# The experts' result stores issued by POOL, those of the last two positions by ScalarE and SP in turn

## The chip, the cores and the metric

One core of a Trainium2 chip runs the program. The metric is the device time of one execution in microseconds, as the median of several runs. Engines are PE (TensorE), DVE (VectorE), ACT (ScalarE), POOL (GpSimd) and SP (SyncE); DMAs are issued here by SP, ACT and POOL.

## What is computed

A decoder block over 1024 tokens of width 1024 in float32: a mixer (half gMLP, half RWKV-7) between two projections, then a mixture of 32 experts in which each token takes its two best experts of its best group, then a last RMSNorm. The part that matters here:

```python
def expert_block(args):
    xbk, e = args
    return (jax.nn.silu(xbk @ w_gate[e]) * (xbk @ w_up[e])) @ w_down[e]

yb = lax.map(expert_block, (xb, block_e)).reshape(P, D)
y = jnp.zeros((N + 1, D), yb.dtype).at[tok_buf].add(yb * w_buf[:, None].astype(yb.dtype))
...
x = x + gate2[:, None, :] * y
...
return _rmsnorm(x, final_norm_g)
```

w_gate and w_up are 1024 x 512 per expert, w_down is 512 x 1024: 6.3 MB of weights for each of 32 experts.

## The kernel before

The mixer and the router take the first 785 us or so. Then comes the experts' stage, which the change touches. The experts are taken in 32 positions; position n has room for CAPS[n] groups of 32 tokens (2 to 6, 90 groups in all), and a Block is up to four groups of one position, 33 blocks in all. A loop over the positions (from L1708 on) runs for position n: weights, `gate_up` of n, `down` of n-1, `act` of n, `operand` of n+1, `gather` of n+2.

- Weights: SP loads each position's gate and up weights (L1471) and down weights (L1478), six DMAs of 1 MB, into a ring of nine tiles `wt` of 2 MB; a load waits until PE is done with the tile's old content.
- `gather` (L1548): POOL issues one indirect DMA per group, which brings token rows from `h2d` into one of three buffers `xg`.
- `operand` (L1556, L1559): DVE transposes `xg` to `xT` and applies scale and shift.
- `gate_up` (L60 by way of `mm_`, into PSUM tiles `mm`, of which there are two): PE multiplies; the groups lie side by side in the 32-column strips of the array. ACT then takes the SiLU into `sg` (L1576), and DVE multiplies it with the up part and the routing weight into `sp` (L1579).
- `act` (L1585): DVE transposes `sp` to `aT`.
- `down` (L60, into PSUM tiles `pch`, three): PE multiplies with the down weights; DVE multiplies by gate2 into one of two buffers `yo` (L1601). Then ACT issues four DMAs that store `yo` to `ysd` in DRAM (L1604), 64 to 128 KB each: 132 in all.

After the loop SP loads `x1d` into two ring tiles (L1743, eight DMAs of 512 KB). A loop for overflowing experts (L1747) follows, which has no iteration with these inputs. Then POOL gathers each token's two result rows from `ysd` with 16 indirect DMAs (L1777); DVE, ACT and POOL add, normalise and scale, and SP and ACT store the output (L1787).

The order of the instructions on each engine is set by the framework's scheduler, which runs the program through a simulated timeline (`schedule_with_timeline_sim=True`); a store may so stand elsewhere than in the code. It also chooses buffers, and gives each DMA a completion semaphore in turn out of a set of eight: DMAHW0 to 7 for the DMAs that SP and ACT issue, DMASW0 to 7 for POOL's. A DMA waits on its issuing engine until the DMA that had the same semaphore before has landed. Each engine runs its instructions in its order.

Of the kernel before, what the change touches and what calls it, by code (L numbers as in the profile page):

```python
# [28 lines left out]
NEXP = 32  # L29
# [25 lines left out]
def hybrid_block(ctx, tc, a, out):  # L55
    nc = tc.nc
    ctx.enter_context(nc.allow_non_contiguous_dma(reason="column layouts"))

    def mm_(*a_, **k_):
        nc.tensor.matmul(*a_, **k_)  # L60
# [22 lines left out]
    def c512():  # L83
        return psc.tile([P, 512], F32, name="pch")
# [164 lines left out]
    class Stream:  # L249


        def __init__(self):
            self.jobs, self.raws, self.parts = [], {}, {}
            self.nl = self.ns = 0
            self.eng = [nc.gpsimd]
            self.loads = []
# [1276 lines left out]
    class Block:  # L1533


        def __init__(self, ix, wt, ng, put):
            self.ix, self.wt, self.ng, self.put = ix, wt, ng, put

        turn = 0

# [47 lines left out]
        def down(self, w):  # L1588
            po = [c512() for _ in range(0, self.ng, 2)]
            w3 = w.rearrange("p (k f) -> p k f", k=4)  # L1590
            for k in range(4):
                for g in range(self.ng):
                    for h in range(4):
                        r = slice(32 * h, 32 * h + 32)
                        mm_(po[g // 2][r, (g % 2) * 256:(g % 2) * 256 + 256], self.aT[:, g, 32 * k:32 * k + 32],
                            w3[:, k, 256 * h:256 * h + 256], start=(k == 0 and g % 2 == 0), stop=(k == 3),
                            skip_group_check=True)
            yo = ap_.tile([P, 4, 256], F32, name="yo")
            for g0 in range(0, self.ng, 2):
                m = min(2, self.ng - g0)  # L1600
                nc.vector.tensor_tensor(yo[:, g0:g0 + m, :], po[g0 // 2][:, 0:256 * m].rearrange("p (g f) -> p g f", g=m),  # L1601
                                        gate2.unsqueeze(1).to_broadcast([P, m, 256]), op=OP.mult)
            for h in range(4):
                nc.scalar.dma_start(self.put[:, :, 256 * h:256 * h + 256], yo[32 * h:32 * h + 32, 0:self.ng, :])  # L1604

    slots = lambda r, n: ysd[r:r + 32 * n, :].rearrange("(g t) f -> t g f", t=32)

# [5 lines left out]
                self.blocks.append(Block(lambda g, g0=g0: idx[:, g0 + g, i:i + 1], lambda g, g0=g0: wrep[:, g0 + g, i:i + 1], n, slots(BASES[i] + 32 * g0, n)))  # L1613

    positions = [Position(i) for i in range(NEXP)]
    for ps_ in positions[0:2]:
        for b_ in ps_.blocks:
            b_.gather()
# [202 lines left out]
```

## Time and profile before

| | us |
|---|---|
| median of 3 runs | 1407.06 |
| lowest and highest of them | 1404.6, 1409.46 |
| the profiled execution | 1394.24 |
| its span, first to last instruction | 1392.4 |
| PE busy (matmul) | 1185.6 |
| DVE busy | 639.5 |
| POOL busy | 468.3 |
| ACT busy | 349.0 |

The profiled execution is a run of its own, 1.8 us longer than its span. Busy times are sums over the whole span, most of which the change does not touch; issuing a DMA does not count as busy time. A row with ACTq or SPq is the engine's queue at issuing DMAs: its duration covers a series of issues together with what they wait for.

### The profile page before, as it was taken

Reading aid. Unit: us, or ns where it says so; the run is one execution under the profiler, and the core shown is the slowest. Engines: PE = TensorE matmul, PEld = TensorE weight load, DVE = VectorE, ACT = ScalarE, POOL = GpSimd, SP = SyncE. Lnnn points to the kernel's source line nnn. Section 1 sums busy time; section 2 is a strip of 40 time slices with the busy share of each in tenths; the row PEclk is TensorE's granted clock in tenths of the full one; section 3 lists DMA queues with packets and bytes.
Section 4 is the critical chain, followed back from the end, with each engine's and each line's share of the span. In section 5 each row is a group of like instructions: output and inputs, shape, how many; then the busy total and the mean of one; then the engine's idle time right before and its main releaser. Section 6 shows DMA issues by size and latency. Waiting matters only on the chain. (4 is left out here: it accounts for less than half of the span.)

```text
span 1392.4 us, 35836 instructions
## 1 busy us (share of the span) xinstructions
PE 1185.6 (85%) x15245; PEld 907.4 (65%) x15245; DVE 639.5 (46%) x1569; ACT 349.0 (25%) x627; POOL 468.3 (34%) x562
## 2 busy tenths in 40 slices
PE   3888799999998899899998489998989999699730
PEld 1576687767875787789986368765657777356420
DVE  2562864793365945772247344332233322132127
ACT  2643453234353643322345200000000000000002
POOL 4464432632554424432440363221122221020025
PEclk9998869999999959899998599999999999899875
DMA  9338325353226212340059799999999999999947
GB/s 324 88 108 296 108 64 175 103 158 90 77 88 191 83 32 65 89 143 32 22 194 387 280 371 416 405 415 405 407 415 393 420 414 411 417 419 359 372 152 278
DMA packets 125139, 336.54 MB, mean 242 GB/s; under 512 B 16936, under 2 KB 77280, under 8 KB 100400
## 3 DMA queue, kind: packets, MB, share of 16 engines
q1 hardware_dynamic: 88784, 273.44, 51.8%
q0 software_dynamic: 13392, 37.63, 7.4%
q10 hardware_dynamic: 22800, 23.12, 5.0%
q8 instruction: 122, 2.00, 0.6%
q14 instruction: 41, 0.34, 0.1%
HBM read 297.98 MB, written 38.96 MB: 242 GB/s over the span
## 5 line engine op out<-in xcount | busy, mean ns | idle before, releaser
L60 PE MATMUL mm<-wt,xT 128*32 128x256 f32 x5760 | 336.0, 393 | 60.2 <-ACT sg L1576 28.1
L60 PEld LDWEIGHTS mm<-wt,xT 128*32 128x32 f32 x5760 | 227.9, 114 | 162.6 <-ACT sg L1576 51.3
L60 PE MATMUL mm<-h,w 128*128 128x512 f32 (+2 forms) x864 | 225.2, 413 | 9.7 <-ACT h L307 4.4
L1548 POOL DMA_INDIRECT xg<-h2d,idx x90 | 98.9, 1099 | 334.0 <-DVE xT L1556 309.7
L60 PEld LDWEIGHTS mm<-h,w 128*128 128x128 f32 (+2 forms) x864 | 161.5, 192 | 56.2 <-issue 6.1
L285 POOL TENSOR_TENSOR w<-wraw,w 128x512 fp32r<-128x512 f32 (+2 forms) x104 | 131.3, 1265 | 141.7 <-ACT w L283 141.2
L60 PE MATMUL pch<-wt,aT 128*32 128x256 f32 x2880 | 162.5, 379 | 2.2 <-DVE yo L1601 2.2
L1579 DVE SCALAR_TENSOR_TENSOR sp<-mm,wrep,sg 128x128 f32<-128x128 f32 x90 | 31.8, 422 | 271.5 <-ACT sg L1576 271.2
L60 PEld LDWEIGHTS pch<-wt,aT 128*32 128x32 f32 x2880 | 111.3, 110 | 46.8 <-DVE yo L1601 3.5
L1576 ACT ACTIVATE sg<-mm 128x256 f32<-128x256 f32 (+1 forms) x52 | 17.1, 354 | 489.3 <-DMA wt<-in_moe_w_up_dram 185.2
L60 PE MATMUL mm<-w,h 128*128 128x256 f32 (+1 forms) x816 | 128.0, 312 | 1.4 <-DVE aw L335 0.5
L60 PEld LDWEIGHTS mm<-w,h 128*128 128x128 f32 x816 | 113.5, 206 | 9.3 <-issue 2.9
L283 ACT ACTIVATE w<-wraw 128x512 fp32r<-128x512 f32 (+2 forms) x104 | 63.4, 615 | 107.5 <-PE mm L60 47.2
L1556 DVE STREAM_TRANSPOSE xT<-xg 128x768 f32<-128x768 f32 (+2 forms) x33 | 29.5, 894 | 89.5 <-PE mm L60 77.7
L60 PE MATMUL pch<-s,GM 16*32 16x16 f32 (+3 forms) x1280 | 53.7, 200 | 6.2 <-DVE s L672 3.4
L60 PEld LDWEIGHTS pch<-s,GM 16*32 16x32 f32 (+2 forms) x1280 | 48.6, 125 | 13.9 <-issue 6.5
L1559 DVE TENSOR_TENSOR xT<-xT,mod 128x768 f32<-128x768 f32 (+2 forms) x66 | 56.7, 859 | 0.2
L1777 POOL DMA_INDIRECT wt<-ysd,rowi x16 | 16.5, 1033 | 101.1 <-DMA ysd<-yo 96.5
L60 PE MATMUL py<-aw,ccol 128*1 128x256 f32 x320 | 28.6, 441 | 11.7 <-DMA aw<-in_ada_w_dram 11.4
L559 DVE SCALAR_TENSOR_TENSOR GM<-pch,nsq,gmask 128x128 f32<-128x128 f32 x128 | 35.2, 341 | 1.6 <-PE pch L60 1.2
L1601 DVE TENSOR_TENSOR yo<-pch,gate 128x512 f32<-128x512 f32 (+1 forms) x52 | 30.0, 608 | 11.1 <-PE pch L60 7.4
L60 PE MATMUL pch<-AR,kb 64*128 64x128 f32 x256 | 28.2, 322 | 4.5 <-DVE GM L559 3.6
(424 smaller groups left out, 1592.2 us busy)
## 6 DMA issues: line engine op xcount, KB each, us to landing
wt<-in_moe_w_gate_dram SPq DMA_DIRECT2D x64, 1024.0 KB
wt<-in_moe_w_up_dram SPq DMA_DIRECT2D x64, 1024.0 KB
wt<-in_moe_w_down_dram SPq DMA_DIRECT2D x64, 1024.0 KB
aw<-in_ada_w_dram SPq DMA_DIRECT2D x48, 512.0 KB
wraw<-in_w_in_dram SPq DMA_DIRECT2D x80, 256.0 KB
ysd<-aw POOLq DMA_DIRECT2D x1, 8192.0 KB, 28.2
ysd<-yo ACTq DMA_DIRECT2D x56, 96.0 KB
wraw<-in_w_out_dram SPq DMA_DIRECT2D x16, 256.0 KB
```

What stands on the lines that cost most here:

```text
L60: nc.tensor.matmul(*a_, **k_)
L283: nc.scalar.activation(hi, raw, AF.Copy)
L285: eng.tensor_tensor(lo, raw, hi.bitcast(F32), op=OP.subtract)
L559: nc.vector.scalar_tensor_tensor(GM[:, u, :], pgs[h][:, c * P:(c + 1) * P], nsq[:, u:u + 1], gmask, op0=OP.mult, op1=OP.mult)
L1548: tc.keep_in_program_order(nc.gpsimd.indirect_dma_start(out=self.xg[:, 256 * g:256 * g + 256], out_offset=None, in_=h2q, in_offset=bass.In ...
L1556: nc.vector.transpose(xT.rearrange("p g k t -> p (g k t)"), self.xg[:, 0:256 * self.ng])
L1559: Block.last = nc.vector.tensor_tensor(xT, xT, m_, op=op)
L1576: nc.scalar.activation(sg[:, g0:g0 + m, :], v[:, :, 0, :], AF.Silu)
L1579: nc.vector.scalar_tensor_tensor(self.sp[:, g0 + g, :].rearrange("p (b j) -> p j b", b=4), perm(v[:, g, 1, :]), self.wt(g0 + g), perm(sg[: ...
L1601: nc.vector.tensor_tensor(yo[:, g0:g0 + m, :], po[g0 // 2][:, 0:256 * m].rearrange("p (g f) -> p g f", g=m), gate2.unsqueeze(1).to_broadca ...
L1777: nc.gpsimd.indirect_dma_start(out=part(t, j), out_offset=None, in_=ysd, in_offset=bass.IndirectOffsetOnAxis(ap=rowi[:, t, j:j + 1], axis=0))
```

## The change

The stores of `yo` to `ysd` at the end of `down` (L1604 before, L1605 now) are issued by the engine that the block names in `eng`. For the blocks of positions 0 to 29 that is POOL, 124 stores. The blocks of the last two positions, 30 and 31, have none: their stores are issued by ACT and SP in turn, two each per position, and so are those of the overflow loop. Nothing else in the code changes; the scheduler makes the order anew.

```diff
@@ class Block
             self.ix, self.wt, self.ng, self.put = ix, wt, ng, put
+            self.eng = None
@@ Block.down
             for h in range(4):
-                nc.scalar.dma_start(self.put[:, :, 256 * h:256 * h + 256], yo[32 * h:32 * h + 32, 0:self.ng, :])
+                (self.eng or (nc.scalar, nc.sync)[h % 2]).dma_start(self.put[:, :, 256 * h:256 * h + 256], yo[32 * h:32 * h + 32, 0:self.ng, :])
@@ after the positions are made
     positions = [Position(i) for i in range(NEXP)]
+    for ps_ in positions[:NEXP - 2]:
+        for b_ in ps_.blocks:
+            b_.eng = nc.gpsimd
```

On ACT, the last rows ahead of the overflow loop before the change (`sg` is the SiLU, `ysd<-yo` a store; 2, 3 or 4 in the middle of its shape is the number of groups):

```order
L1604 DMA ysd<-yo 32x3x256 x4
L1576 ACTIVATE sg<-mm 128x256
L1604 DMA ysd<-yo 32x4x256 x4
L1604 DMA ysd<-yo 32x2x256 x4
L1576 ACTIVATE sg<-mm 128x256
L1576 ACTIVATE sg<-mm 128x128
L1576 ACTIVATE sg<-mm 128x256 x2
L1604 DMA ysd<-yo 32x3x256 x4
L1604 DMA ysd<-yo 32x2x256 x4
L1604 DMA ysd<-yo 32x3x256 x4
L1604 DMA ysd<-yo 32x2x256 x4
```
The same place now. The stores of positions up to 29 are gone from between the SiLUs; what is left are two of position 30:

```order
L1577 ACTIVATE sg<-mm 128x128
L1577 ACTIVATE sg<-mm 128x256 x4
L1577 ACTIVATE sg<-mm 128x128
L1577 ACTIVATE sg<-mm 128x256 x2
L1577 ACTIVATE sg<-mm 128x128
L1577 ACTIVATE sg<-mm 128x256 x2
L1605 DMA ysd<-yo 32x2x256 x2
```
What a store waits for on ACT before the change, at the eight stores in a row with a SiLU ahead and behind (the row of waits names semaphores and engines):

```order
L1576 ACTIVATE sg<-mm 128x256 [waits PE_49,Activation_49]
L1604 DMA ysd<-yo 32x4x256 [waits DMAHW4_49,DVE_49]
L1604 DMA ysd<-yo 32x4x256 [waits DMAHW5_49]
L1604 DMA ysd<-yo 32x4x256 [waits DMAHW6_49]
L1604 DMA ysd<-yo 32x4x256 [waits DMAHW7_49]
L1604 DMA ysd<-yo 32x2x256 [waits DMAHW0_49,DVE_49]
L1604 DMA ysd<-yo 32x2x256 [waits DMAHW1_49]
L1604 DMA ysd<-yo 32x2x256 [waits DMAHW2_49]
L1604 DMA ysd<-yo 32x2x256 [waits DMAHW4_49]
L1576 ACTIVATE sg<-mm 128x256 [waits PE_49,Activation_49]
```
Each has to wait for a semaphore of the set that SP's weight loads use as well. On POOL, the last rows ahead of the overflow loop were gathers alone:

```order
L1548 DMA xg_8154<-h2d,idx 128x256 x2
L1548 DMA xg_8155<-h2d,idx 128x256 x3
L1548 DMA xg_8156<-h2d,idx 128x256 x2
L1548 DMA xg_8154<-h2d,idx 128x256 x2
L1548 DMA xg_8155<-h2d,idx 128x256 x2
L1548 DMA xg_8156<-h2d,idx 128x256 x2
```
Now the stores stand between them; the stores of three more positions follow behind these rows:

```order
L1605 DMA ysd<-yo 32x3x256 x4
L1549 DMA xg_8156<-h2d,idx 128x256 x2
L1605 DMA ysd<-yo 32x4x256 x4
L1605 DMA ysd<-yo 32x2x256 x4
L1549 DMA xg_8154<-h2d,idx 128x256 x2
L1549 DMA xg_8155<-h2d,idx 128x256 x2
L1605 DMA ysd<-yo 32x3x256 x4
L1549 DMA xg_8156<-h2d,idx 128x256 x2
L1605 DMA ysd<-yo 32x2x256 x4
L1605 DMA ysd<-yo 32x3x256 x4
L1605 DMA ysd<-yo 32x4x256 x4
L1605 DMA ysd<-yo 32x2x256 x4
```
At the end of the stage DVE's last four results were these before, with their waits; the last one waits for the semaphores of the stores of position 29, whose buffer it takes:

```order
L1601 TENSOR_TENSOR yo<-pch,gate_7481 128x512 [waits DMAHW2_49,DMAHW4_49,DMAHW1_49,DMAHW0_49]
L1585 STREAM_TRANSPOSE aT<-sp 128x256 [waits DVE_49,PE_49]
L1601 TENSOR_TENSOR yo<-pch,gate_7481 128x512 [waits DMAHW6_49,DMAHW1_49,DMAHW7_49,DMAHW0_49,DVE_49]
L1601 TENSOR_TENSOR yo<-pch,gate_7481 128x256
L1601 TENSOR_TENSOR yo<-pch,gate_7481 128x512 [waits DMAHW3_49,DMAHW4_49,DMAHW2_49,DMAHW5_49,DVE_49,PE_49]
L1601 TENSOR_TENSOR yo<-pch,gate_7481 128x512 [waits DMAHW1_49,DMAHW6_49,DMAHW0_49,DMAHW7_49,DVE_49,PE_49]
```
Now those of positions 28, 29 and 30 wait for POOL's stores two positions back, and the last one waits for four semaphores of the other set, which are those of position 30's stores:

```order
L1602 TENSOR_TENSOR yo<-pch,gate_7481 128x512 [waits DMASW6_49,DMASW7_49,DMASW5_49,DMASW4_49]
L1586 STREAM_TRANSPOSE aT<-sp 128x256 [waits DVE_49,PE_49]
L1602 TENSOR_TENSOR yo<-pch,gate_7481 128x512 [waits DMASW2_49,DMASW1_49,DMASW3_49,DMASW0_49,DVE_49]
L1602 TENSOR_TENSOR yo<-pch,gate_7481 128x256
L1602 TENSOR_TENSOR yo<-pch,gate_7481 128x512 [waits DMASW5_49,DMASW6_49,DMASW4_49,DMASW7_49,DVE_49,PE_49]
L1602 TENSOR_TENSOR yo<-pch,gate_7481 128x512 [waits DMAHW1_49,DMAHW6_49,DMAHW0_49,DMAHW7_49,DVE_49,PE_49]
```
These are issued by ACT (two) and by SP, where the two stand behind the eight loads of `x1d`; each waits for the semaphore of one of those loads:

```order
L1747 DMA wt<-x1d 128x1024 [waits DMAHW6_49,PE_49]
L1747 DMA wt<-x1d 128x1024 [waits DMAHW7_49]
L1747 DMA wt<-x1d 128x1024 [waits DMAHW0_49]
L1747 DMA wt<-x1d 128x1024 [waits DMAHW1_49]
L1747 DMA wt<-x1d 128x1024 [waits DMAHW2_49,DMASW6_49,PE_49]
L1747 DMA wt<-x1d 128x1024 [waits DMAHW3_49,DMASW7_49]
L1747 DMA wt<-x1d 128x1024 [waits DMAHW4_49,DMASW0_49]
L1747 DMA wt<-x1d 128x1024 [waits DMAHW5_49,DMASW1_49]
L1605 DMA ysd<-yo 32x2x256 [waits DVE_49,DMAHW7_49,Activation_49,Pool_49]
L1605 DMA ysd<-yo 32x2x256 [waits DMAHW0_49]
```
## Rows read from the trace of the kernel before

**Rows 1.** The page, part 2: the span in 40 equal slices of 34.8 us, the DMA engines' busy tenths and the GB/s that they moved.

```profile
DMA  9338325353226212340059799999999999999947
GB/s 324 88 108 296 108 64 175 103 158 90 77 88 191 83 32 65 89 143 32 22 194 387 280 371 416 405 415 405 407 415 393 420 414 411 417 419 359 372 152 278
```

**Rows 2.** Busy time by stage, one row for a stretch (us from the span's start): its length, busy us of PE, PEld, DVE, ACT and POOL with the count of records, then granted clock, DMA share, GB/s.

```profile
810.00:1260.00 450.00, 414.51 (x7424) 294.58 (x7420) 140.95 (x274) 16.04 (x46) 102.47 (x93) 0.96 1.02 411
1060.00:1070.00 10.00, 10.00 (x192) 7.32 (x188) 4.69 (x11) 0.77 (x2) 3.13 (x4) 1.00 0.96 323
1130.00:1140.00 10.00, 10.00 (x192) 7.29 (x187) 0.00 (x0) 0.00 (x0) 0.00 (x0) 1.00 1.01 418
1260.00:1280.00 20.00, 18.49 (x334) 11.15 (x330) 7.55 (x15) 1.03 (x3) 0.00 (x0) 1.00 0.85 314
1280.00:1302.00 22.00, 17.29 (x323) 12.29 (x312) 2.04 (x4) 0.00 (x0) 0.00 (x0) 0.98 1.02 421
1302.00:1310.00 8.00, 4.69 (x45) 2.51 (x49) 3.12 (x7) 0.55 (x2) 0.00 (x0) 0.50 0.66 227
1308.00:1310.00 2.00, 2.00 (x25) 1.00 (x21) 0.00 (x0) 0.00 (x0) 0.00 (x0) 0.50 0.94 340
```

**Rows 3.** The timeline of ACT and its queue in the experts' stage: start us, duration us, engine, line, operation, out<-in, count, and in brackets the idle time before with its releaser.

```profile
1014.63 11.65 ACTq L1604 DMA_DIRECT2D ysd<-yo  x4
1026.38 0.38 ACT L1576 ACTIVATE sg<-mm 128x256 f32<-128x256 f32 x1 [16.17 <-DMA wt<-in_moe_w_up_dram]
...
1188.11 8.57 ACTq L1604 DMA_DIRECT2D ysd<-yo  x4
1196.77 0.38 ACT L1576 ACTIVATE sg<-mm 128x256 f32<-128x256 f32 x1 [21.17 <-DMA wt<-in_moe_w_up_dram]
1204.15 13.51 ACTq L1604 DMA_DIRECT2D ysd<-yo  x4
1217.76 0.55 ACT L1576 ACTIVATE sg<-mm 128x256 f32<-128x256 f32 x2 [20.60 <-DMA ysd<-yo]
...
1286.68 17.32 ACTq L1604 DMA_DIRECT2D ysd<-yo  x8
1304.10 0.55 ACT L1576 ACTIVATE sg<-mm 128x256 f32<-128x256 f32 x2 [26.14 <-DMA ysd<-yo]
...
1340.16 2.26 ACTq L1604 DMA_DIRECT2D ysd<-yo  x4
```

**Rows 4.** The timeline of PE's matmuls from 1176 us to its last one, same columns.

```profile
1176.26 7.11 PE L60 MATMUL mm<-wt,xT 128*32 128x256 f32 x128 [0.61 <-ACT sg L1576]
...
1198.03 11.65 PE L60 MATMUL mm<-wt,xT 128*32 128x256 f32 x176 [8.61 <-DVE sp L1579]
...
1218.97 15.74 PE L60 MATMUL mm<-wt,xT 128*32 128x256 f32 x256 [5.83 <-ACT sg L1576]
...
1305.31 16.94 PE L60 MATMUL mm<-wt,xT 128*32 128x256 f32 x256 [8.02 <-ACT sg L1576]
1323.99 12.29 PE L60 MATMUL pch<-wt,aT 128*32 128x256 f32 x224 [1.75 <-DVE yo L1601]
```

**Rows 5.** Who waited for whom: PE from 810 to 1345 us, then SP's queue from 1180 to 1345 us (line, who was waited for: us in total, times, longest us).

```profile
PE mm L60 <- ACT sg L1576: 28.1, 8, 8.0
PE mm L60 <- DVE sp L1579: 15.9, 5, 8.6
...
SPq L1478 <- DMA wt<-in_moe_w_down_dram: 21.5, 1, 21.5
SPq L1471 <- PE pch L60: 8.4, 1, 8.4
```

**Rows 6.** The timeline of SP's queue from 1306 us, of DVE's last result and of POOL's first gather of the last stage, same columns as in group 3.

```profile
1306.21 0.86 SPq L1478 DMA_DIRECT2D wt<-in_moe_w_down_dram  x2
1307.17 6.96 SPq L1743 DMA_DIRECT2D wt<-x1d  x8
...
1336.56 0.69 DVE L1601 TENSOR_TENSOR yo<-pch,gate 128x512 f32<-128x512 f32 x1 [2.97 <-PE pch L60]
...
1346.96 0.97 POOL L1777 DMA_INDIRECT wt<-ysd,rowi  x1 [96.49 <-DMA ysd<-yo]
```

**Rows 7.** The chain of waits that ended last, in order of time, from 1342 to 1348 us: start us, us, what.

```profile
1341.93 4.38 DMA ysd<-yo
...
1347.93 0.30 issue
```

**Rows 8.** POOL's issues by line: the gathers L1548 from 860 to 1260 us (operation, count: ns min/median/max; next row: us to landing), then the direct DMAs of 512 KB from POOL's queue at L1107 with their landings, and the stretch in which these landed, with the columns of group 2.

```profile
L1548 POOL DMA_INDIRECT xg<-h2d,idx x62: 992/1000/1742, 861.3 to 1249.1; - x62
...
DMA to landing us min/median/max: 5.7/6.8/8.2
...
L1107 POOL DMA_DIRECT2D h2d<-b x4: 531/531/576, 764.2 to 773.2; - x4
...
DMA to landing us min/median/max: 16.6/16.7/17.3
...
764.00:790.00 26.00, 16.71 (x171) 13.27 (x170) 11.98 (x72) 9.48 (x13) 3.89 (x8) 0.65 0.90 363
```

**Rows 9.** The page, part 5: PE's groups of the experts' stage (line, engine, operation, out<-in, count | busy us, mean ns of one | idle us before, releaser).

```profile
L60 PE MATMUL mm<-wt,xT 128*32 128x256 f32 x5760 | 336.0, 393 | 60.2 <-ACT sg L1576 28.1
L60 PE MATMUL pch<-wt,aT 128*32 128x256 f32 x2880 | 162.5, 379 | 2.2 <-DVE yo L1601 2.2
```

## The prediction

> **What bounds the kernel now.** The page's slices come first [rows 1]: from slice 24 (801 us) on the DMA engines are busy nine tenths or more, at 371 and then 393 to 420 GB/s; slices 37 and 38 fall to 359 and 372, the next to 152, and there the last stage begins. The busy times by stage say it closer [rows 2]: 411 GB/s from 810 to 1260 us (418 in an undisturbed stretch, some 415 between its dips), but 314 from 1260 to 1280 and 227 from 1302 to 1310. A position brings 6 weight loads of 1.049 MB, and on average 2.8 gathers of 131 KB and as many bytes of results: 7.0 MB, at 415 GB/s 16.9 us. PE has 8640 records in 32 positions [rows 9], 270 each; at 192 in 10 us [rows 2] that is 14.1 us. So the DMA stream is the limit, and PE can catch up 2.8 us per position.
>
> Then ACT and its queue [rows 3]. The four stores of a position hold ACT for 8.6 to 13.5 us, and the SiLU stands right behind them: it starts 0.1 us after the last store's issue, though its matmuls are long done. The order printed above tells why: each store waits for a semaphore DMAHW that a weight load of SP had before it. Against 0.5 us for an issue that finds its semaphore free (2.26 us for four at 1340), the rest is waiting for loads. PE pays: 28.1 us before matmuls that wait for the SiLU, 15.9 for the product behind it [rows 5]. Up to 1180 us most of this is covered by the DMA stream. From there it is not: PE stands 8.61, 5.83 and 8.02 us [rows 4], the ring of weight tiles fills, SP waits 8.4 us for PE [rows 5], and the stream has holes. At the very end eight stores in a row hold ACT 17.32 us, and SP's load of the last down weights waits 21.5 us for another load [rows 3, 5]. PE's last matmul ends at 1336.28; from the last result to the end the kernel runs a fixed chain.
>
> **The change, part by part.**
> *ACT loses 124 of 132 issues.* The SiLU then follows its matmuls. Two limits tell what this gives at the end of PE's work. PE's own: from 1176 us it loses 8.61 + 5.83 + 8.02 = 22.5 us standing, and runs slower behind each stand (the granted clock is 0.50 from 1302 to 1310 us, its level of 1.2 GHz, after the longest [rows 2]): 176 records in 11.65 us, 256 in 15.74 and 256 in 16.94 [rows 4] instead of 9.8, 14.2 and 14.2 at 55.5 ns (128 in 7.11), 6.1 us more. Together 28.6 us. The weights': the holes cost (415-323) x 10, (415-314) x 20 and (415-227) x 8, over 415: 2.2 + 4.9 + 3.6 = 10.7 us [rows 2]. The last two loads were issued from 1306.21 us on [rows 6]; 0.68 MB by 1310 at 340 GB/s and 1.42 MB at 415 make them land at about 1313.4. Without holes: 1302.7. The last gate and up weights stand 4 loads ahead, 10.1 us: 1292.6. Behind them come 64 records (3.6 us), the gap of 1.75 us for SiLU and product, and the 224 records of the last three down products (12.29 us) [rows 4]: 1310.2 instead of 1336.28, so **-26.1 us**. The smaller of the two is taken. Earlier than 1176 us nothing is counted: there the stream hides ACT.
>
> *POOL gains 124 issues.* A direct DMA takes 0.53 to 0.58 us of POOL, the gap to the next issue 0.30 us, a gather 1.00 [rows 7, 8]. Per position: 4 x 0.85, 2.8 x 1.30 and half a table scatter at a gather's price, 0.65: 7.7 us of 16.9. In the printed order stores and gathers alternate; a gather is issued some two positions ahead of its use, so a store that waits in front of it for its result holds nobody. Cost 0, hidden by POOL's idle time; if that cover goes, it is the last rival. The results are in two buffers, so DVE's result n+2 waits until store n has landed: 4 issues (up to 5.2 us, at the 1.00 us of a gather) and a landing as of a gather, 5.7 to 8.2 us [rows 8], 13 us of 34. Cost 0. The bytes stay the same, so the stream's rate does.
>
> *The last two positions.* Two issues by ACT and two by SP instead of four in a row: of 2.26 us half goes, **-1.1 us** before the gathers at 1346.96 [rows 3, 6]. Against it stands a new wait, seen in the order only: the last result now takes the buffer of the one before it, so DVE waits until the stores of position 30 have landed. SP issues its two of them behind eight loads of x1d (4.19 MB). Before, these loads were issued at 1307 to 1314 [rows 6] and long gone; now they follow the last weights directly and end at 1302.7 + 10.1 = 1312.8 us. With 2 us for the landing (between 0 and the 4.38 of the chain [rows 7]) the last result starts at 1314.8 instead of 1310.2: **+4.6 us**, bounds 0 and 8 (both issues and a full landing behind the last load). Behind that result DVE has only the last stage, which POOL starts when the stores of position 31 have landed. A faster PE so runs into transfers that it never met.
>
> Sum: -26.1 - 1.1 + 4.6 = **-22.6 us**. On the profiled execution (1394.24 us) that is 1371.6. The median of the runs is 12.8 us above it, so the difference is laid on the median: 1407.06 - 22.6 = **1384.5 us**.
>
> Here a rule speaks against it. By the rows, an issue held ACT not for the cost of issuing but for its wait. The Trainium skill, "DMA: Bandwidth & Descriptors", section "Issuing engines are not separate DMA queues", says that DMAs of all issuers share the same 16 DMA engines, and that issuing from several engines saves only the sequencer's issue time. By that rule the sum would be the -1.1 us of the last issues. The rows agree with its first half (the bytes and 415 GB/s stay); for its second half 17.32 us of ACT for eight stores is the other measure.
>
> **The rivals.**
> *Only the last stand goes.* The weights may bring PE's lateness back: SP's loads wait for semaphores in turn, and PE may stand for weights where it stood for the SiLU. Then only the 8.02 us, the 2.7 us of slow matmuls behind it and the 1.1 us go, and the last result waits for an undisturbed landing, +2.7 (a result 0.69, two issues 1.13, landing 4.38, less the 3.5 us that PE's last 64 records take anyway): -9.1 us, **1398 us**. For it: most stands before 1176 us cost nothing. Against: SP waited 8.4 us for PE, not PE for weights.
>
> *No change.* The stream ends when it ends and the last weights set the finish; the holes would be the loads' own. 1407.06 - 1.1 = **1406 us**. Against it: the holes lie where PE stood.
>
> *POOL becomes the bound, and it is slower.* POOL's DMAs take their semaphores DMASW from a set of eight, in turn; an issue waits until the DMA eight before has landed. A position has 7.2 of them (230 in 32), so POOL keeps pace while a landing takes less than 8 / 7.2 x 16.9 = 18.8 us. At 20 us a position takes 18.0, 1.1 more, in 28 positions 31 us; less the 9.1 above it is +22: **1429 us**. The place is the gather behind held stores, then DVE's transpose. For it: four direct DMAs of 512 KB landed after 16.6 to 17.3 us while loads ran beside them [rows 8]. Against: the stores have 96 KB, and gathers among saturated loads landed after 8.2 us at most. The Trainium skill, "SBUF — State Buffer", section "SBUF: two separate sides", names another way there: POOL can't write descriptors while VectorE runs a two-port operation, 620 ns becoming 3100. By that the estimate is 2.5 us more per store, 17.7 us of POOL per position, and some 1420 us; the trace's longest gather issue is 1.742 against 1.000 us [rows 8].
>
> **How the numbers follow.** The forecast has 0.68, only the last stand 0.16, no change 0.08, POOL as bound 0.08. The low end is PE's own limit without the new wait, 28.6 + 1.1: 1377.4, less 2.4 for the spread of the three runs, 1375. The high end holds the first rival with the same spread: 1400. What is left out are the last two cases. A measurement can tell 0.3% from no change, about 4 us: faster 0.84, same 0.08, slower 0.08.
>
> **What would show it.** Right: ACT's SiLUs wait for PE alone, PE's three stands after 1176 us are gone, the DMA rate stays near 415 GB/s until the last weights at about 1303 us, the last result starts near 1315 with DVE waiting for a store of position 30, and the stage of the gathers keeps its 45 us. Wrong: DVE waiting for stores in the middle of the stage, POOL's landings above 15 us, PE standing for weights after 1180 us, or a rate below 405 GB/s before it.

## The result and the profile after

The changed kernel takes **1398.33 us** (median of 8 runs, 1392.39 to 1402.11), the kernel before 1405.55 beside it (8 runs, 1400.97 to 1409.46): a ratio of **0.9937 [0.9916, 0.9958]**. It is faster, as forecast, but by 7.2 us here, and by 10.4 and 9.7 us in two later sets of runs, instead of 22.6. Four of the versions below had one execution each of 1736 to 6191 us, far above their others, which their ratios leave out.

The profiled execution of the change took 1399.25 us, 5.0 us *more* than that of before in [rows 1 to 9]. The reason is where the experts' stage starts: its first SiLU is at 816.30 us there and at 835.25 us in the change. A second profile of the kernel before starts at 832.50 us, and one of the change at 832.00, so this is a difference between executions. What sets it was not settled, but it goes with the chip: the seven profiles of groups 3 and 4 below, all from one chip, start at 813 to 820 us, the other eleven, from three chips, at 823 to 839. With the early start the kernel before also took 5 us longer from there (520.0 us from the first SiLU to PE's last matmul when it starts at 816, 515.2 us when it starts at 832). So times are counted from the first SiLU below, and the second profiles of both kernels, which start alike, are what is subtracted.

The slices of the change, as those of [rows 1]. The stage has no slice of 359 or 372 GB/s at its end any more; there is one of 380, which holds a hole that is left, then 419, in which `x1d` follows the last weights:

```profile
DMA  9338326353236202241059769999999999999965
GB/s 323 87 110 299 104 64 186 90 171 84 69 92 204 71 25 75 78 142 31 17 191 391 284 214 407 417 416 416 420 415 419 420 418 419 419 417 380 419 212 217
```

Busy time by stage in the same execution, columns as in [rows 2], then 10 us of it by themselves. POOL went from 102 us to 157 in the long stretch (on POOL, other than on SP and ACT, issuing a DMA does count as busy time). Up to 1321 us the stream moves 413 to 420 GB/s on average, with one hole in it, 288 GB/s from 1270 to 1280 us. PE's granted clock (column before the DMA share) is 1.00, 1.00, 0.92 and 1.00, and 0.83 in the hole; the 0.50 from 1302 to 1310 us, behind PE's longest stand, has no counterpart:

```profile
829.00:1279.00 450.00, 433.54 (x7680) 333.41 (x7676) 149.53 (x288) 18.23 (x49) 156.73 (x188) 1.00 1.01 414
1279.00:1299.00 20.00, 20.00 (x376) 12.03 (x372) 4.56 (x10) 0.66 (x2) 4.32 (x8) 1.00 1.01 413
1299.00:1321.00 22.00, 17.88 (x299) 11.05 (x294) 4.06 (x10) 0.77 (x2) 0.55 (x2) 0.92 1.01 420
1321.00:1329.00 8.00, 7.75 (x144) 5.17 (x136) 0.51 (x2) 0.00 (x0) 3.73 (x8) 1.00 0.96 379
```
```profile
1270.00:1280.00 10.00, 7.74 (x112) 4.37 (x116) 3.08 (x7) 0.00 (x0) 2.17 (x4) 0.83 0.76 288
```

Who waited for whom from 810 to 1345 us, ACT first, then PE, as [rows 5]. ACT's SiLU waits for PE alone. Of PE's 28.1 us for the SiLU 3.5 are left (16.9 and 4.4 in the second profiles, which start alike). Waits for `yo`, which frees a PSUM tile, grow from 2.2 us to 6.5, and waits for weights are new. "issue" is time in which PE waited for nothing that the profile shows; in the second profile of the kernel before it is 10.0 us too, so it does not come with the change:

```profile
ACT sg L1577 <- PE mm L60: 464.6, 37, 26.7
```
```profile
PE mm L60 <- issue: 10.3, 8, 2.2
PE pch L60 <- DVE yo L1602: 6.5, 3, 3.2
PE mm L60 <- DMA wt<-in_moe_w_up_dram: 4.9, 4, 2.4
PE mm L60 <- ACT sg L1577: 3.5, 3, 2.2
```

PE's last matmuls in that execution, as [rows 4]. The stands of 8.61, 5.83 and 8.02 us are gone; the longest now is 3.25:

```profile
1272.26 8.80 PE L60 MATMUL pch<-wt,aT 128*32 128x256 f32 x128 [3.25 <-DVE yo L1602]
...
1309.34 8.80 PE L60 MATMUL mm<-wt,xT 128*32 128x256 f32 x128 [2.38 <-DMA wt<-in_moe_w_up_dram]
1319.88 8.86 PE L60 MATMUL pch<-wt,aT 128*32 128x256 f32 x160 [1.74 <-DVE yo L1602]
1329.72 3.66 PE L60 MATMUL pch<-wt,aT 128*32 128x256 f32 x64 [0.98 <-PE pch L60]
```

Behind it the last results on DVE, then POOL's first gather of the last stage, as [rows 6]. The last result stands 6.45 us and starts 4.4 us behind PE's end (1333.38); before, it started 0.3 us behind it. The row books the wait to SP at the overflow loop (L1751). The semaphores that the result waits for, though, are those of position 30's four stores, and the last of these landed at 1337.65 us by its increments, just ahead of the result:

```profile
1328.93 1.02 DVE L1602 TENSOR_TENSOR yo<-pch,gate 128x512 f32<-128x512 f32 x2 [3.15 <-DMA ysd<-yo]
1330.68 0.69 DVE L1602 TENSOR_TENSOR yo<-pch,gate 128x512 f32<-128x512 f32 x1 [0.72 <-DMA ysd<-yo]
1337.82 0.69 DVE L1602 TENSOR_TENSOR yo<-pch,gate 128x512 f32<-128x512 f32 x1 [6.45 <-SPq L1751]
```
```profile
1346.22 1.04 POOL L1781 DMA_INDIRECT wt<-ysd,rowi  x1 [13.80 <-DMA ysd<-yo]
```

The pair that starts alike, kernel before and then the change: PE's last matmuls of the second profiles.

```profile
1306.29 3.66 PE L60 MATMUL pch<-wt,aT 128*32 128x256 f32 x64
1318.01 15.69 PE L60 MATMUL mm<-wt,xT 128*32 128x256 f32 x256 [8.05 <-ACT sg L1576]
1335.45 12.29 PE L60 MATMUL pch<-wt,aT 128*32 128x256 f32 x224 [1.75 <-DVE yo L1601]
```
```profile
1305.82 8.74 PE L60 MATMUL mm<-wt,xT 128*32 128x256 f32 x128 [3.27 <-DMA wt<-in_moe_w_up_dram]
1316.31 8.86 PE L60 MATMUL pch<-wt,aT 128*32 128x256 f32 x160 [1.75 <-DVE yo L1602]
1326.24 3.66 PE L60 MATMUL pch<-wt,aT 128*32 128x256 f32 x64 [1.07 <-issue]
```

PE ends at 1347.74 and 1329.90: 17.8 us earlier. The first gather comes at 1358.10 and 1342.69: 15.4 us earlier. The span ends at 1404.0 and 1394.4: only 9.6 us earlier. So 5.8 us are lost *behind* the first gather, in a stage that the change does not touch. The last waits of SP tell where (line, who was waited for: us in total, times, longest), and POOL's own row at that line what (count: ns min/median/max). Before, then the change:

```profile
SPq L1817 <- DMA out_dram<-wt: 2.2, 1, 2.2
SPq L1817 <- PEq L1817: 0.7, 2, 0.5
```
```profile
L1817 POOLq DRAIN  x3: 46/111/1817, 1398.1 to 1403.8; - x3
```
```profile
SPq L1821 <- PEq L1821: 6.6, 2, 6.0
SPq L1821 <- DMA out_dram<-wt: 2.0, 2, 1.6
```
```profile
L1821 POOLq DRAIN  x3: 46/111/10718, 1382.8 to 1394.1; - x3
```

The waits name PE's queue, which has nothing to do there. What is late is POOL: at the closing barrier its DRAIN takes 10.72 us instead of 1.82.

### The profile page after: what moved, and what is told of

Read it like the earlier page. It is cut to its first block, busy times and chain, and to the rows that moved or that the text cites. A ratio compares the mean times of both kernels' runs of the same rounds, so it can differ in the third digit from the quotient of the medians.

```text
span 1397.5 us, 35829 instructions
## 1 busy us (share of the span) xinstructions
PE 1201.7 (86%) x15245; PEld 943.3 (67%) x15245; DVE 639.1 (46%) x1569; ACT 350.4 (25%) x627; POOL 543.0 (39%) x686
## 5 line engine op out<-in xcount | busy, mean ns | idle before, releaser
L60 PE MATMUL mm<-wt,xT 128*32 128x256 f32 x5760 | 339.3, 385 | 34.7 <-DVE xT L1560 13.2
L60 PEld LDWEIGHTS mm<-wt,xT 128*32 128x32 f32 x5760 | 250.3, 111 | 112.8 <-issue 46.2
L1549 POOL DMA_INDIRECT xg<-h2d,idx x90 | 103.7, 1152 | 243.6 <-DVE xT L1557 208.4
L60 PE MATMUL pch<-wt,aT 128*32 128x256 f32 x2880 | 181.4, 382 | 9.7 <-DVE yo L1602 6.5
L60 PEld LDWEIGHTS pch<-wt,aT 128*32 128x32 f32 x2880 | 124.4, 111 | 57.8 <-issue 17.1
L60 PEld LDWEIGHTS mm<-w,h 128*128 128x128 f32 x816 | 116.3, 211 | 9.5 <-issue 3.0
L1605 POOL DMA_DIRECT2D ysd<-yo x124 | 69.2, 571 | 101.9 <-DVE yo L1602 101.8
L60 PE MATMUL py<-aw,ccol 128*1 128x256 f32 x320 | 28.1, 434 | 12.2 <-DMA aw<-in_ada_w_dram 11.9
```

Of the source, the lines that this page charges most:

```text
L1549: tc.keep_in_program_order(nc.gpsimd.indirect_dma_start(out=self.xg[:, 256 * g:256 * g + 256], out_offset=None, in_=h2q, in_offset=bass.In ...
L1605: (self.eng or (nc.scalar, nc.sync)[h % 2]).dma_start(self.put[:, :, 256 * h:256 * h + 256], yo[32 * h:32 * h + 32, 0:self.ng, :])
```

## The experiments

They ran in five groups, each beside its own runs of the kernel before (medians 1391.84 to 1406.11 us), so ratios of one group are compared. The table has, from each trace: the first SiLU of the experts, from there to the end of PE's last matmul, from that to the first gather of the last stage, from that to the end, and POOL's closing DRAIN (us). "Stores" is how many POOL issues.

| group, kernel | stores | ratio [95%] | first SiLU | to PE's end | to gather | to end | DRAIN |
|---|---|---|---|---|---|---|---|
| 1 before_again | 0 | 0.9988 [0.9964, 1.0011] | 832.50 | 515.25 | 10.36 | 45.90 | 1.82 |
| 1 after_again | 124 | 0.9904 [0.9867, 0.9940] | 832.00 | 497.90 | 12.79 | 51.71 | 10.72 |
| 1 pool_only | 124 | 0.9928 [0.9902, 0.9954] | 827.70 | 498.25 | 13.20 | 51.74 | 10.72 |
| 1 last_only | 0 | 0.9984 [0.9959, 1.0009] | 838.87 | 517.94 | 8.28 | 45.40 | 1.81 |
| 2 drain_early | 124 | 0.9926 [0.9907, 0.9945] | 831.31 | 499.49 | 16.98 | 46.12 | 1.96 |
| 2 yo31_own | 124 | 0.9921 [0.9899, 0.9943] | 836.67 | 507.36 | 4.18 | 51.59 | 10.72 |
| 2 all_pool | 132 | 0.9888 [0.9870, 0.9905] | 830.24 | 498.39 | 12.85 | 44.02 | 1.49 |
| 2 half_pool | 60 | 0.9996 [0.9981, 1.0011] | 831.32 | 516.87 | 8.58 | 46.72 | 5.90 |
| 3 late_pool | 24 | 0.9955 [0.9922, 0.9988] | 813.53 | 513.72 | 9.87 | 45.58 | 3.53 |
| 3 early_pool | 100 | 0.9993 [0.9965, 1.0022] | 817.91 | 518.83 | 8.88 | 49.68 | 8.76 |
| 3 pool31 | 128 | 0.9919 [0.9892, 0.9947] | 815.82 | 503.97 | 7.33 | 51.58 | 11.04 |
| 3 yo24_first | 124 | 0.9936 [0.9910, 0.9962] | 820.23 | 499.55 | 13.01 | 51.02 | 10.72 |
| 4 small26 | 124 | 0.9966 [0.9942, 0.9989] | 813.36 | 504.96 | 13.59 | 51.40 | 10.72 |
| 4 all_yo24 | 132 | 0.9931 [0.9903, 0.9958] | 819.81 | 501.62 | 11.67 | 45.40 | 1.49 |
| 4 pool31_yo24 | 128 | 0.9928 [0.9906, 0.9951] | 815.25 | 502.14 | 7.20 | 51.91 | 11.04 |
| 5 after_third | 124 | 0.9927 [0.9901, 0.9952] | 827.54 | 497.49 | 12.82 | 51.55 | 10.72 |
| 5 all_pool_b | 132 | 0.9899 [0.9869, 0.9929] | 823.13 | 498.32 | 12.84 | 45.92 | 1.49 |
| 5 all_yo24_b | 132 | 0.9895 [0.9866, 0.9924] | 831.70 | 500.52 | 11.86 | 45.03 | 1.49 |

### Both kernels again, and the change in halves

Two copies, and each half of the change alone:

```diff
pool_only:  (self.eng or nc.scalar).dma_start(...)   # last two positions by ACT
last_only:  b_.eng = nc.scalar                       # positions 0 to 29 by ACT
```

> The kernel before, unchanged, profiled a second time. Theory A (the profile of before that was shown began its expert stage early, and that is rare): the first SiLU of the experts now starts at 825 to 837 us instead of 816.30, the profiled time is 1401 to 1409 instead of 1394.24, and the stage from there on looks as before. Theory B (the late start of the changed kernel, first SiLU at 835.25, comes with the change): the first SiLU again at 814 to 820 us, profiled time 1392 to 1397. Timed runs: ratio 1.00 under both.

> The changed kernel, unchanged, profiled a second time. Theory A: the first SiLU lies anywhere from 816 to 837 us, and the time moves with it; PE's late arrival at the closing barrier (6.0 us in the first profile) comes and goes. Theory B: again at 833 to 837 us, with the 2 us gaps of PE between 810 and 822, and PE again 6 us late at the end. Timed runs: 1396 to 1401 us under both, 0.992 to 0.996 of before.

> POOL issues the stores of positions 0 to 29 as in the change; the stores of the last two positions are all issued by ACT, as before. If the gain comes from the 124 stores that ACT loses, nearly all of it is here: 1396 to 1402 us, between 1 us faster and 3 us slower than the change (the two issues that go back to ACT cost 1.1 us; SP's two stores behind eight x1d loads go away, up to 4.4 us back). If the gain came from the last two positions alone: 1403 to 1407 us.

> ACT and SP issue the stores of the last two positions in turn as in the change; all others stay with ACT. If the gain comes from the 124 stores: 1402 to 1409 us, the last stand halved or replaced by the wait for SP's stores. The rival, that only the last stand of PE counts: 1396 to 1400 us, as fast as the change.

The kernel before can start its stage at 832.5 us too, so the late start does not come with the change. The whole gain is POOL's half: pool_only has the change's 498 us up to PE's end, last_only before's 518. The last two positions' issues by ACT and SP are worth nothing that can be measured.

### The DRAIN and the last result

```diff
drain_early:  tc.keep_in_program_order(nc.gpsimd.drain())   # ahead of the loads of x1d
yo31_own:     yo = xgs[1]... for the last block             # a buffer of its own
all_pool:     for ps_ in positions:                         # all 132 stores by POOL
half_pool:    positions[:NEXP - 2:2] by POOL, positions[1:NEXP - 2:2] by ACT
```

> The change, with one more DRAIN of POOL right behind its last store (position 29), where POOL then waits 11 to 14 us for the gathers. In the three profiles with POOL's stores the closing DRAIN takes 10.72 us and ends 5.9 us after everything else; in the three without them 1.82 us, and it holds nobody. Theory (POOL's DRAIN has to settle the DMAs that POOL issued, once): the early one takes 8 to 11 us between 1328 and 1342, the closing one falls to about 2 us, from the first gather to the end 45.4 to 46 us instead of 51.3 to 51.7, time 1389 to 1393 us (6 us less than the change). Rival (the closing DRAIN has its length from the number of direct DMAs in the whole program, or from something else at the end): still 10.7 us, no gain, or a loss of up to 5 us if the early one delays the first gather.

> The change, with the last position's result in a tile of its own (the gather tile of position 31, which has been transposed by then) instead of the buffer of position 30's result. It tests the step of +4.6 us: the last result should then follow PE's last matmul at once instead of standing 6.4 us behind SP's branch and position 30's stores. First gather 8.0 to 9.5 us behind PE's end instead of 12.8 and 12.8: time 1391 to 1395 us. Rival (the landing of position 31's stores behind the x1d loads takes the time anyway): no change, 1396 to 1400.

> All 132 stores by POOL, the last two positions' too. Their issue stands behind no x1d load, but four issues in a row take 2.2 us on POOL against 0.9 on ACT and SP side by side. First gather 10 to 14 us behind PE's end; the closing DRAIN 11 us if its length goes with the number of direct DMAs on POOL (84 ns each), 10.7 if not. Time 1394 to 1400 us.

> POOL issues the stores of every second position of 0 to 29 (60 DMAs), ACT those of the others; the last two by ACT and SP. It asks for two doses. The closing DRAIN of POOL: about 6 us if its length goes with the number of stores on POOL, 1.8 or 10.7 if it is a matter of yes or no. PE's end behind the first SiLU (515 to 520 us with ACT, 498 with POOL): 505 to 512 if every store that ACT loses counts alike, 498 to 501 if ACT has only to be free every second position. Time 1396 to 1404 us.

drain_early: POOL's rows at its own DRAIN and at the closing one.

```profile
L1745 POOLq DRAIN  x1: 10183/10183/10183, 1329.0 to 1329.0; - x1
```
```profile
L1821 POOLq DRAIN  x3: 46/111/1962, 1388.2 to 1393.6; - x3
```

The 10 us are owed for the stores and paid once: the closing DRAIN falls to 1.96 us and the last stage to 46.12, as before. But the early one held POOL to 1339.2 us, ACT came through the overflow loop's barrier only behind POOL and issued its stores of the last position from 1342.7 us (1337.2 in the change's second profile), and the first gather came 4 us later. Net gain: none that shows, against 6 us expected.

half_pool's DRAIN (5.90 us for 60 stores) fits 72 ns per store, (10.72 - 1.82) / 124, within 0.3 us; so do late_pool, early_pool and pool31 below. Whether it goes with the stores' number or their bytes was not separated. **all_pool breaks the line**: with 132 stores it is 1.49 us. Why it falls between 128 and 132 is open. It is the one version here that keeps the change's 498 us and not its 5.8.

yo31_own took the wait for position 30's stores away, and won nothing: the scheduler then put PE's last eight records behind the empty overflow loop, whose barrier waits in its turn. SiLU to gather is 511.5 us, 511.0 in the change.

```profile
1342.95 1.08 PE L60 MATMUL pch<-wt,aT 128*32 128x256 f32 x8 [6.13 <-issue]
```

half_pool gains nothing: from the first SiLU to the first gather it takes 525.5 us, before_again 525.6. The fifteen positions whose stores stay on ACT are enough to keep the holds. Behind the one of 13.24 us PE stands 7.5 us. At the end four stores stand ahead of the last SiLU for another 4.05 us, and PE stands 6.90 us, a wait that the profile puts down to nobody:

```profile
1214.64 13.24 ACTq L1605 DMA_DIRECT2D ysd<-yo  x4
...
1332.28 4.05 ACTq L1605 DMA_DIRECT2D ysd<-yo  x4
1336.43 0.38 ACT L1577 ACTIVATE sg<-mm 128x256 f32<-128x256 f32 x1 [16.23 <-DMA wt<-x1d]
```
```profile
PE mm L60 <- ACT sg L1577: 11.1, 4, 7.5
```
```profile
1338.70 9.50 PE L60 MATMUL pch<-wt,aT 128*32 128x256 f32 x128 [6.90 <-issue]
```

### Which positions matter

```diff
late_pool:   b_.eng = nc.gpsimd if positions.index(ps_) >= 24 else nc.scalar
early_pool:  b_.eng = nc.gpsimd if positions.index(ps_) < 24 else nc.scalar
pool31:      for ps_ in positions[:NEXP - 1]:
yo24_first:  tc.issue_after(<the yo of position 24>) around gate_up of 28 and operand of 30
```

> POOL issues only the stores of positions 24 to 29; those of 0 to 23 stay with ACT, the last two positions are shared by ACT and SP as in the change. It asks where PE's time comes from. If only the last stands count (the rival 'only the last stand goes'): PE's end 498 to 503 us behind the first SiLU, as in the change, and a closing DRAIN of 1.8 to 3 us, so 1391 to 1396 us. If the free SiLU counts over the whole stage: 508 to 516 us, time 1399 to 1405.

> The counterpart: POOL issues the stores of positions 0 to 23, ACT those of 24 to 29. If only the last stands count: PE's end 514 to 520 us behind the first SiLU, as before, and 1404 to 1409 us. If the stage as a whole counts: 502 to 508 us, 1396 to 1401. The closing DRAIN: 8 to 9 us if its length goes with the stores on POOL (5.9 us at 60, 10.72 at 124), then 3 to 4 us of it are on the path.

> POOL issues the stores of positions 0 to 30, ACT and SP share those of the last one alone: 128 stores on POOL. With 124 the closing DRAIN took 10.72 us, with 132 it took 1.49. It places the turn: 11.0 us if it lies above 128, 1.2 to 1.5 if below. The last result waits for position 30's stores by POOL as in the run with all on POOL (3.7 us behind PE's end instead of 4.4); its own issue takes 0.9 us instead of 2.1. With the short DRAIN 1387 to 1391 us, with the long one 1394 to 1399.

> The change, with position 24's result moved on DVE ahead of the product of position 28 and the operand of position 30, the only difference in the order of any engine. In the change PE stands 3.25 us for that result and the DMA rate falls to 329 GB/s from 1270 to 1280 us (385 and 398 beside it), 3.4 us of stream. Theory (the forecast counted all holes of the stream as gone, and this one stays because it comes from DVE's order): the rate stays above 410 GB/s there and PE's end comes 2 to 4 us earlier, 495 us behind the first SiLU instead of 498. Rival (PE stands for something else there, or behind the last weights the gain is lost): PE's end at 497.5 to 498.5, no change of the time.

late_pool frees ACT only from position 24 on. The stand at 1303 us goes, the two around 1190 to 1220 stay:

```profile
1197.53 12.32 PE L60 MATMUL mm<-wt,xT 128*32 128x256 f32 x176 [8.65 <-DVE sp L1580]
...
1218.46 16.41 PE L60 MATMUL mm<-wt,xT 128*32 128x256 f32 x256 [5.16 <-ACT sg L1577]
```

early_pool is the other way round, and worse: ACT's last stores and the SiLU behind them, and PE behind that.

```profile
1260.82 45.17 ACTq L1605 DMA_DIRECT2D ysd<-yo  x12
...
1306.09 0.55 ACT L1577 ACTIVATE sg<-mm 128x256 f32<-128x256 f32 x2 [48.34 <-DMA wt<-in_moe_w_down_dram]
```
```profile
1307.31 15.37 PE L60 MATMUL mm<-wt,xT 128*32 128x256 f32 x256 [20.69 <-ACT sg L1577]
```

Twelve stores hold ACT 45.17 us. An issue costs about half a us, and for some 5 us the next result is not there yet (DVE ends it at 1269.3 us); the rest is waiting for loads that use the same eight semaphores. With like (early) starts PE's end behind the first SiLU is 520.0 us before, 513.7 in late_pool, 518.8 in early_pool and 504.0 in pool31, which has the stores of both stretches and of position 30 on POOL: 6 and 1 us won apart, 16 together, each from one profile; the ratios say the same. **The stands do not add up**: a place that is left brings most of the lateness back. So neither of the two theories put up for these runs held: not the last stands alone, and not every store alike. pool31's first gather comes 7.33 us behind PE's end instead of some 12.8, but it has the long DRAIN too, and its ratio can't be told from the change's.

In yo24_first DVE's `yo` of position 24 is put ahead of `xT` of position 30. It had stood behind it and kept a PSUM tile from PE. The hole in the weights' stream closes (the change's second profile, then yo24_first):

```profile
1260.00:1290.00 30.00, 26.75 (x499) 16.63 (x492) 8.27 (x15) 0.38 (x1) 6.48 (x12) 1.00 0.94 371
```
```profile
1270.00:1280.00 10.00, 10.00 (x192) 7.31 (x188) 1.21 (x4) 0.66 (x2) 0.00 (x0) 1.00 1.02 422
...
1295.93 8.56 PE L60 MATMUL mm<-wt,xT 128*32 128x256 f32 x128 [6.82 <-DMA wt<-in_moe_w_up_dram]
```

and PE pays at the next place: 6.82 us for the last up weights instead of 3.27. The ratio is the change's; the 3 us expected did not come.

### The spread of a load's landing, and the best versions

```diff
small26:      loads of positions from 26 on cut in two (512 KB each)
all_yo24:     all_pool and yo24_first together
pool31_yo24:  pool31 and yo24_first together
```

> The change, with the weight loads of the last six positions cut in two (0.5 MB instead of 1 MB each, the same bytes): eight loads in flight are then 4 MB, 10 us of stream, instead of 20. Theory (the lag of the slowest DMA engine over the bytes, 9.3 us between the first and the last increment of the last weight loads, delays PE's last position): the increments of the last loads lie within 2 to 5 us, the last weights land 4 to 6 us closer to their bytes, PE's end comes 3 to 6 us earlier: 492 to 495 us behind a late first SiLU (827 us or later; 498 in the change), 498 to 501 behind an early one (below 822; 504 with 31 positions on POOL), time 3 to 5 us below the change's ratio of 0.990 to 0.994. Rival (PE itself, its order and its clock, sets the end): the increments move together but PE's end stays within 1.5 us.

> All 132 stores on POOL (the closing DRAIN took 1.5 us there instead of 10.7) together with position 24's result first on DVE (PE's end 4.4 us earlier than without). If the two add up: ratio to the kernel before 0.983 to 0.987, PE's end 493 to 495 us behind a late first SiLU or 498 to 500 behind an early one, 44 to 46 us from the first gather to the end. If the gain of the order is lost behind the last weights: 0.987 to 0.990, as with the stores alone.

> Stores of positions 0 to 30 on POOL, the last one's by ACT and SP, with position 24's result first on DVE. With the stores alone the ratio was 0.992, of it 6 us for the closing DRAIN of 11 us; the first gather came 7.3 us behind PE's end instead of 12.8. If the order adds its 4.4 us: 0.987 to 0.990, the DRAIN again 11 us. It is slower than all on POOL if the DRAIN counts more than the last stores (6 against 5.5 us: within 2 us of each other).

A load lands when the last of the 16 increments of its semaphore has come. The first and last of them lie 0.9 us apart at the last loads of the kernel before and 8.0 in the change. In small26 the last gate and up loads have 6.9 us, and take 11.4 us from issue to landing (1280.70 to 1292.08) where one of the last loads of the change takes 21 (1292.02 to 1313.06). Yet the last of them landed no earlier: 486.1 us behind the first SiLU, against 484.1 in the kernel before and 483.5 in pool31 with equally early starts, and PE ended at 505.0, as in pool31 (504.0). The ratio, 0.9966, is no better than the change's. So the theory that smaller loads would bring the landing forward fell. As I read it, a load that is issued later for less time in flight still lands when the stream's slowest engine gets to it.

The copies for the final comparison, all in one group:

> The change, unchanged, beside the two versions below. Ratio 0.990 to 0.994 as in its first two sets of runs; closing DRAIN 10.7 us, 51 to 52 us from the first gather to the end. The last position's up weights land 479 us behind a late first SiLU or 483 behind an early one, PE's last matmul ends 19 to 20.5 us behind them (34.7 to 35.9 in the kernel before).

> All 132 stores on POOL, again. If the closing DRAIN is worth its 5.9 us: 4.5 to 7.5 us faster than the change in this call, ratio lower by 0.003 to 0.0055, DRAIN 1.5 us. If its short DRAIN was luck of one profile: as fast as the change.

> All 132 stores on POOL with position 24's result first, again. If the order counts beside the DRAIN: 1 to 4 us faster than with the stores alone. If the last weights take the gain back: within 1 us of it.

after_third 1395.91 us, all_pool_b 1391.92, all_yo24_b 1391.95 (before 1405.62). all_pool is the best version that was found, some 4.0 us faster than the change. In this group the two intervals overlap (0.9899 and 0.9927); what carries it is also its mechanism: 5.6 us of last stage (45.92 against 51.55). Moving `yo` of position 24 as well adds nothing: 0.9895 here, and only 0.9931 for all_yo24 in group 4, where 0.983 to 0.987 was hoped for.

## Why the prediction came out as it did

The forecast's sum beside the pair that starts alike:

| term | forecast | measured |
|---|---|---|
| end of PE's last matmul | -26.1 | -17.8 |
| from there to the first gather (-1.1 + 4.6) | +3.5 | +2.4 |
| from the first gather to the end | 0 | +5.8 |
| sum | -22.6 | -9.6 |

**The step that failed is "Without holes: 1302.7".** It took the holes in the rate as time by which the weights' *landing* moves. The bytes did as forecast: counted over the weights' queue, the last weights' bytes were through 11.2 us earlier (forecast 10.7), though one hole stayed. The landings did not. First and last increments of the last gate or up load and of the last down load (read from the semaphores' updates, us):

| | before_again | after_again | earlier by |
|---|---|---|---|
| last gate/up load, first increment | 1310.7 | 1302.6 | 8.1 |
| last gate/up load, last increment (landed) | 1313.0 | 1310.6 | 2.4 |
| last down load, first increment | 1325.7 | 1312.5 | 13.2 |
| last down load, last increment | 1326.6 | 1320.6 | 6.0 |

Under the long full stream the 16 DMA engines drift apart: first and last increment of a weight load lie 5 us apart in the middle of the stage in the kernel before, and 14 to 15 us from 1200 to 1250 us in the change (means). Before, the eight semaphores were shared by 6 loads and 4 stores per position, so some 4.8 loads were in flight; now all eight are loads. At 2.5 us for 1 MB that is 12 and 20 us, and from issue to landing a load takes about 11 and 21 us (medians). So the stores' waits also paced the loads. late_pool and early_pool, from one group, show both regimes: from 900 to 1200 us 4.3 loads are in flight and the spread is 5.6 us where ACT issues the stores, 7.8 and 14.0 us where POOL does (means). As I read it, the "holes" were mostly idle time of the engines that were ahead: where these no longer idle, bytes come earlier, but a load is done when its slowest engine is. The forecast's 7.8 us came for the first increment of the last gate and up load (8.1), and the growth of the spread from 2.3 to 8.0 us took 5.7 of it. The runs with position 24's result first bear this out: with the hole smaller (371 instead of 329 GB/s from 1270 to 1280 us), in all_yo24_b, that load's first increment comes 2.3 us earlier behind the first SiLU than in after_again (468.3 against 470.6), its last 1.8 later (480.4 against 478.6), the spread being 12.1 us. small26 has half the bytes in flight from position 26 on, and its spread from 1200 to 1250 us is 6.9 us instead of 14.4; so the spread goes with the bytes in flight, and the last landing does not. What makes some engines slower is open: the trace does not tell them apart, and in every run with eight loads of 1 MB in flight POOL issued the stores. The Trainium skill, "DMA: Bandwidth & Descriptors", section "Why a DMA increments its semaphore by 16 and not by 1", says that the engines of one DMA finish independently and that only the full count means landed; the trace agrees, with 8.0 us between the first and the last.

In numbers: the forecast moved the last gate and up load by 7.8 us (1300.4 measured in the first profile to 1292.6); it moved 2.4, **5.4 us short**. Behind it the forecast had 17.64 us; it is 19.3, **1.7 short**, of which 1.07 is a gap between the last two down products that did not stand in the sum. And at a like start before's PE ends 34.7 us behind that load, not 35.9: 1.2. Together 8.3, the difference between -26.1 and -17.8.

**The term that was put at nothing** is the DRAIN: +5.8 us. "The stage of the gathers keeps its 45 us" was wrong. The forecast costed POOL's stores at nothing because POOL has idle time. That held for their issue, but not for what POOL settles at the end. drain_early, which pays it ahead, and all_pool, where it is 1.49 us, have last stages of 46.1 and 44.0 us.

**What was right.** ACT's SiLU waits for PE alone and PE's three stands are gone. Two of the forecast's own signs of being wrong came too: PE stands for weights after 1180 us (2.38 and 3.27 us for the last up weights), and the rate falls below 405 GB/s once (288 from 1270 to 1280 us). The new wait of the last result was named and came: it starts 4.4 us behind PE's end (forecast 4.6). That the size fits is luck, for its cause is another. SP was through with `x1d` at 1324.5 us, and SP and ACT issued position 30's stores side by side as soon as the result was there, from 1331.4; what takes the time is their landing, 6.2 us. In pool_only, where SP issues none of them, the way to the gather is as long (13.20 us). What this wait is worth by itself stays open: yo31_own took it away and won nothing, but there PE's last records stand behind the overflow loop's barrier.

**The rivals.** *Only the last stand goes* named 1398 us, the measured time, and its reason came true in part: weights bring some of the lateness back. Its sum did not: all three stands went, PE ends 17.8 us earlier, not 10.7, and the DRAIN, which it does not have, takes 5.8 back. late_pool, which removes just the last stand, gets 6 of 16 us. So that the number fits is luck. *POOL becomes the bound* did not come: its stores take 536 to 647 ns to issue and land in 4.9 to 9.4 us, gathers in 5.6 to 7.9, and DVE waits for stores only from 1278 us on (5.3 us in 3 waits, and the last result's):

```profile
L1605 POOL DMA_DIRECT2D ysd<-yo x124: 536/567/647, 851.5 to 1328.4; - x124
```
```profile
L1549 POOL DMA_INDIRECT xg<-h2d,idx x90: 945/1032/2084, 791.2 to 1246.3; - x90
```

The longest gather issue is 2.08 us; the 3100 ns that the Trainium skill, "SBUF — State Buffer", section "SBUF: two separate sides", gives for a DMA of POOL that VectorE holds up shows in no issue. Whether VectorE ran an operation of the kind that holds POOL up beside one, the rows do not tell. *No change* fell as well: by the second half of the rule of "Issuing engines are not separate DMA queues" (the Trainium skill, "DMA: Bandwidth & Descriptors") only -1.1 us should come; the trace disagrees, with -17.8 us at PE's end. What the issuing engine paid here was for the most part the wait for a semaphore, in the 45.17 us of twelve issues as elsewhere.

## What to carry to other kernels

An issue that waits for a shared completion semaphore holds everything behind it on its engine; move it to an engine with nothing urgent behind, and to another set of semaphores (the change did both at once, and no run separates them), but for every position, since one place left can bring all the lateness back. Do not read a hole in the rate as time that the last load will gain: look at when its last semaphore increment comes, and what share of the DMAs in flight are loads. When work moves to an engine, look at that engine's rows at the very end of the program too: what it settled there was on the path here.

## What the runs showed of the hardware

- POOL's closing DRAIN grows with the direct DMAs that POOL issued: 1.82 us without the stores, 3.53, 5.90, 8.76, 10.72 and 11.04 us with 24, 60, 100, 124 and 128 of them, and 1.49 us with 132 (four profiles). Where it is late, the waits name PE's queue.
- The 16 increments of one weight load lie 0.9 us apart at the end of the kernel before and 8.0 us in the change, there in two halves: eight within 0.9 us, the other eight 3.3 to 8.0 us behind the first. With more bytes in flight the DMA engines drifted further apart, and the last landing moved little (2.4 and 6.0 us).
- The experts' stage starts at 813 to 839 us in executions of nearly the same program: at 813 to 820 us in all seven profiles from one chip, at 823 to 839 in the eleven from three others. Why the chips differ is open.
